# Query norms by transposes instead of matrix products with a column of ones, and small products that are issued at once

## The chip, the core and the metric

The kernel runs on one core of a Trainium2 chip. The metric is the device time of one execution in microseconds (us). Before the change the median of 3 runs is 856.51 us (855.76 to 857.1). The work is split over five engines: TensorE (PE; its weight loads are shown apart as PEld), VectorE (DVE), ScalarE (ACT), GpSimd (POOL) and SyncE (SP, which issues the transfers).

## The reference

One decoder layer: 256 tokens of width 2048, float32, and 256 memory tokens. One input projection gives queries and keys (12 heads of 128 each), values (24 heads of 128), two gate columns per value head, the queries of a cross-attention into the memory tokens, and a SiLU gate of width 4096. The first mixer is a gated DeltaNet; the part that the change touches is its output:

```python
q = jnp.repeat(l2_norm(q), rep, axis=2) * DN_HEAD_DIM ** -0.5
k = jnp.repeat(l2_norm(k), rep, axis=2)
...
o = gated_delta_rule(q, k, v, g, beta)
o = rms_norm(o.astype(p.dtype), out_g)
...
y = jnp.concatenate([mix, xa], axis=-1) * jax.nn.silu(z)
x = x + jnp.einsum("bse,ed->bsd", y, w_out[i])
```

The query enters the delta rule linearly, so its norm can be applied after it: the sum of squares of a query goes into the mean square of the output row by which the output is divided.

## The kernel before, in words

**The stream.** The projections are one long list of weight tiles (`PLAN`): memory values and keys, the gate columns, and then tiles of the kinds x, k, z, v, q and o, 273 in all. Each tile of 512 KB is fetched from memory, rounded by ScalarE to a high part (line 342, `CAST wt<-st`), and VectorE subtracts this from the tile and keeps the rest as a low part (line 346, `wt<-st,wt`). TensorE then multiplies high by high, high by low and low by high (tiles `pa` and `pb` in PSUM; 128x512 or 128x256 products). There are four buffers for prepared tiles (`wt`) and five for raw ones (`st`).

**The small products.** Everything else is a Python generator that runs beside the stream: convolutions, Gram matrices, the inverse of the triangular matrices, the delta rule in six groups of two query heads and four value heads (`delta(g)`), and the transposes of the gated result for the output projection (`split_y`). The builder keeps a clock of its own (`now`) and adds a modelled duration to it for each product (`mm`, `tr`). A generator that wants TensorE next yields `"pe"` with a time, `gather`; it is put on the list `waiting`. After each few products of the stream `step_side` looks at that list: once one entry's time has come, all entries on the list are advanced together. Before, the five requests of a delta group wait up to 0.5 us of the builder's clock for others (`GATHER`), and the transposes of `split_y` up to 4.0 us (`GATHER_Y`). Gram matrices, the cross-attention and the inverse ask with 0.0. Instructions that are issued before 45 us of the builder's clock are pinned to the order of the program; later ones may be moved by the framework's own scheduler, for which the program's order is a rank.

**One delta group.** It takes five rounds on TensorE: (1) keys by keys and queries, `pkq`; (2) the inverse by the first half of the values, `pU`; (3) state products `pU` and the first half's outputs `pO`; (4) the same `pU` and `pO` for the second half; (5) the second half's outputs `pO` and, beside them, the query norms `pqs`. For the norms ScalarE squares the queries of the two heads (`q2`, shown in the trace as `q<-kq`, 128x256 each), and four float32 products with a column of ones sum each over its 128 features: the squared queries are the weights, the column of ones has one column. VectorE reads the four columns from PSUM, adds a small number and scales (`eq`). ScalarE sums the squares of the outputs (`ojunk`), VectorE adds both (`e`), GpSimd raises to the power -1/2, and VectorE scales the outputs and gates them. The PSUM bank of the norms comes from the two banks with the tag `m`.

In the profile every matrix product of the kernel stands under line 86 and nearly every other instruction of the generators under line 103, since helpers issue them. They are told apart by their tiles.

Of the kernel before, what the change touches and what calls it, by code (L numbers as in the profile page):

```python
# [10 lines left out]
AF = mybir.ActivationFunctionType  # L11
ALU = mybir.AluOpType
AX = mybir.AxisListType
# [8 lines left out]
NB = 2  # L22
C = 128
EPS = 1e-6
# [8 lines left out]

LOOK = 2
WARM = 9
GATHER = 0.5
GATHER_Y = 4.0
XPACE = 3.0
HOP = 0.25
PINNED = 45.0  # L40
# [32 lines left out]
def hybrid_kernel(ctx: ExitStack, tc: tile.TileContext, x, xT, memT, W, prm_d, cst_d, out):  # L73
# [32 lines left out]
    def width(ap):  # L106
        n = 1
        for d in ap.shape[1:]:
            n *= d
        return n  # L110
# [14 lines left out]
    ve, se = Engine(nc.vector, ve_cost), Engine(nc.scalar, se_cost)  # L125
# [19 lines left out]
    def S2(name, shape, dt=F32):  # L145
        return s2p.tile([128] + list(shape), dt, name=name, tag="s2")

    def SM(name, shape, bufs=3, dt=F32):
        n = 1
        for d in shape:  # L150
            n *= d
        if n > 128:
            return smp.tile([128] + list(shape), dt, name=name, tag="s1k", bufs=6)
        if n > 16:
            return smp.tile([128] + list(shape), dt, name=name, tag="s512", bufs=3)
        return smp.tile([128] + list(shape), dt, name=name, tag=name, bufs=bufs)
# [7 lines left out]
    def PS(tag, name):  # L164
        idle[tag].remove(min(idle[tag]))
        pt = ps.tile([128, 512], F32, name=name, tag=tag, bufs=PB[tag])
        held[id(pt)] = (tag, pt)
        return pt

    def spare(tag, n=1):  # L170
        return sum(t <= now[0] for t in idle[tag]) >= n

    def give(pt, t):

        idle[held.pop(id(pt))[0]].append(t)

    def bank(tag, name):
        yield from until(lambda: spare(tag))
        return PS(tag, name)

    def banks(name):
        yield from until(lambda: spare("m", 2))
        return [PS("m", name) for _ in range(2)]
# [10 lines left out]
    def mm(o_, lhsT, rhs, start, stop):  # L194
        n = width(rhs)
        if rhs.dtype == F32:
            now[0] += {32: 0.015, 64: 0.038}.get(rhs.shape[0], max(0.19, 4 * n / 2400.0))
        else:
            now[0] += max(0.092, n / 2400.0 + 0.0137) + 0.01 * (n == 256)
        te.matmul(o_, lhsT, rhs, start=start, stop=stop)  # L200

    def tr(o_, i_):
        now[0] += 0.093
        te.transpose(o_, i_, ident)
# [25 lines left out]
    def until(cond):  # L230
        while not cond():
            yield POLL

    def pe_soon(gather=0.0):

        yield max(fin[0] - now[0], 0.0) + SLACK
        yield "pe", gather
# [9 lines left out]
    def calm(queued=CALM):  # L247

        while ve.end > now[0] + queued:
            yield ve.end - now[0] - queued  # L250
# [5 lines left out]
    ones = cst[:, K_ONE : K_ONE + 1]  # L256
# [623 lines left out]
    KQ = [None] * NPAIR  # L880
# [242 lines left out]
    def split_y():  # L1123
        for j0 in (12, 14, 0, 2, 4, 6, 8, 10):
            jj = (j0, j0 + 1)
            yield from until(lambda: all(yf[j] is not None for j in jj))
            yield from calm(0.8)
            yield "pe", GATHER_Y
            pts = yield from banks("pyT")
# [45 lines left out]
    def v_done(g):  # L1175
# [13 lines left out]
        def done(r, pt):  # L1189
            def go():  # L1190
# [41 lines left out]
                if r == 1:  # L1232
                    vss[g] = raw
                    yield from delta(g)
# [8 lines left out]
    def delta(g):  # L1243

        pp = (2 * g, 2 * g + 1)
# [4 lines left out]
        heads = [(w, w // 2, w % 2) for w in range(4)]  # L1250
        yield from pe_soon(GATHER)

# [16 lines left out]
        for i, p in enumerate(pp):  # L1269
            ve.tensor_tensor(out=kcl[:, i], in0=pkv[i][:, 0:4:2, :], in1=kch[:, i], op=ALU.subtract)  # L1270
            give(pks[i], ve.end)
        yield from pe_soon(GATHER)
        A = yield from bank("A", "pU")
# [15 lines left out]
        ve.tensor_tensor(out=ul, in0=u0f, in1=uh, op=ALU.subtract)  # L1289
        yield from pe_soon(GATHER)  # L1290
        yield from until(lambda: spare("A") and spare("B"))
        A, B = PS("A", "pU"), PS("B", "pO")
# [16 lines left out]
        give(B, se.end)  # L1309
        yield from pe_soon(GATHER)  # L1310
        yield from until(lambda: spare("A", 2))
        A, B = PS("A", "pU"), PS("A", "pO")
# [8 lines left out]
        for w in range(4):  # L1321
            se.activation(oq[:, w, :], B[:, w * C : (w + 1) * C], AF.Copy, scale=egc[:, 4 * g + w : 4 * g + w + 1])
        give(B, se.end)
        q2 = S2("q2", [2, 256])
        for i, p in enumerate(pp):
            se.activation(q2[:, i, :], KQ[p][:, 1, :], AF.Square)
        yield from pe_soon(GATHER)
        yield from until(lambda: spare("B") and spare("m"))
        B, pq = PS("B", "pO"), PS("m", "pqs")
        for w, i, h in heads:  # L1330
            mm(B[:, w * C : (w + 1) * C], aT[i][:, 1, h, :], u1[:, w, :], start=True, stop=True)
        for b in range(NB):
            for i in range(2):
                mm(pq[:, 2 * b + i : 2 * b + i + 1], q2[:, i, b * C : (b + 1) * C], ones, start=True, stop=True)
        yield 0.2
        ve.tensor_tensor(out=o[1], in0=B.rearrange("c (h e) -> c h e", h=4), in1=oq, op=ALU.add)
        give(B, ve.end)

        eq, e4 = SM("eq", [4], 2), SM("e4", [3, NB, 4], 2)
        ve.tensor_scalar(out=eq, in0=pq[:, 0:4], scalar1=EPS, scalar2=EPS * 128, op0=ALU.add, op1=ALU.mult)  # L1340
        give(pq, ve.end)
        ready.add(f"d{g}")
        yield
        for b in range(NB):
            for w in range(4):
                junk = SM("ojunk", [C])
                se.activation(junk, o[b][:, w, :], AF.Square, accum_out=e4[:, 0, b, w : w + 1])
        yield
        yield from until(lambda: {f"z{g}0", f"z{g}1"} <= ready)
        ev = [e4[:, a].rearrange("c b (i h) -> c (b i) h", h=2) for a in range(2)]  # L1350
        ve.scalar_tensor_tensor(out=ev[1], in0=ev[0], scalar=1.0 / 128,
# [156 lines left out]
```

## Time and profile before

| | before |
|---|---|
| median of 3 runs | 856.51 us (855.76 to 857.1) |
| the profiled execution, its own time | 857.04 us |
| its span, first to last instruction | 855.3 us |
| PE busy | 848.0 us, 99% |
| PE weight loads busy | 709.7 us, 83% |
| DVE busy | 618.1 us, 72% |
| ACT busy | 538.1 us, 63% |
| POOL busy | 46.5 us, 5% |
| instructions | 13175, of them 4790 matrix products |

Busy time is the union of the intervals in which an engine has an instruction under way. Products on TensorE overlap, so one shown with 390 ns can be followed by the next after 230 ns: what a product costs is read from the starts of two neighbours, not from its duration. A float32 product (two passes) stands in the trace as two records with a weight load each, a transpose as one record.

### The profile page before, as it was taken

The numbers are of one execution on the slowest core, as the hardware profiler recorded it, in microseconds if no ns is written. First come the engines' busy times: TensorE is split into PE (matmuls) and PEld (weight loads), VectorE is DVE, ScalarE is ACT, GpSimd is POOL, SyncE is SP. The second block draws the span as 40 slices with busy tenths as digits, with TensorE's granted clock in tenths as the row PEclk, the third lists the DMA queues.
The fourth block names the chain that finished last, engine by engine and source line by source line (L and its number), as shares of the span: only waits on it lengthen the run. The fifth ranks groups of instructions, "written<-read, shape, count | busy, mean of one in ns | idle before, by whom it ended". The sixth has DMA issues, their size and how long they took to land.

```text
span 855.3 us, 13175 instructions
## 1 busy us (share of the span) xinstructions
PE 848.0 (99%) x4790; PEld 709.7 (83%) x4790; DVE 618.1 (72%) x1080; ACT 538.1 (63%) x929; POOL 46.5 (5%) x45
## 2 busy tenths in 40 slices
PE   9999999999999999999999999999999999999998
PEld 6888888888888888888888888788888888888886
DVE  6878886657779974788889989568886655454442
ACT  7656665798644765995966676679775654333331
POOL 1000000000000000001100202000010000000000
PEclk9999999999999999999999999999999999999999
DMA  9965566448677886869877769686755547666650
GB/s 344 335 218 177 171 189 165 146 147 263 197 208 241 263 243 180 261 210 266 226 243 218 227 214 279 198 242 222 227 158 169 186 142 265 214 210 205 199 197 25
DMA packets 145433, 181.59 MB, mean 212 GB/s; under 512 B 24824, under 2 KB 115824, under 8 KB 145368
## 3 DMA queue, kind: packets, MB, share of 16 engines
q1 hardware_dynamic: 145080, 180.47, 67.0%
q8 instruction: 37, 0.61, 0.3%
q10 hardware_dynamic: 288, 0.28, 0.1%
q14 instruction: 28, 0.23, 0.1%
HBM read 167.58 MB, written 6.89 MB: 204 GB/s over the span
## 4 chain that ended last, share of the span: by engine, by line
PE 95%; ACT 2%; DMA 1%; DVE 1%; issue 1%; SPq 0%; DVEq 0%
PE pb L86 72%; PE pa L86 13%; PE pO L86 2%; PE pU L86 2%; PE pm L86 1%; PE pkq L86 1%; PE pyT L86 1%; ACT dec L103 1%; DVE wt L346 1%; PE pqs L86 1%; PE pkk L86 1%; DMA erow<-dgc 0%; DMA st<-W_d 0%; ACT L103 0%; PE pab L86 0%
## 5 line engine op out<-in xcount | busy, mean ns | idle before, releaser
L346 DVE TENSOR_TENSOR wt<-st,wt 128x1024 fp32r<-128x1024 f32 (+1 forms) x275 | 331.9, 1212 | 164.9 <-ACT wt L342 161.2
L342 ACT CAST wt<-st 128x1024 fp32r<-128x1024 f32 (+1 forms) x275 | 286.3, 1045 | 224.3 <-PE pb L86 180.6
L86 PE MATMUL pb<-wt,hkt 128*128 128x512 f32 x1536 | 361.8, 392 | 0.0
L86 PEld LDWEIGHTS pb<-wt,hkt 128*128 128x128 f32 x1536 | 284.7, 188 | 58.7 <-DVE wt L346 0.4
L86 PE MATMUL pb<-wt,yhi 128*128 128x512 f32 x512 | 158.0, 390 | 0.0
L86 PE MATMUL pa<-hkt,wt 128*128 128x512 f32 (+1 forms) x768 | 142.8, 342 | 0.4 <-DVE wt L346 0.3
L86 PEld LDWEIGHTS pa<-hkt,wt 128*128 128x128 f32 x768 | 117.9, 188 | 18.3 <-DVE wt L346 1.0
L86 PEld LDWEIGHTS pb<-wt,yhi 128*128 128x128 f32 x512 | 95.7, 188 | 19.6
L86 PE MATMUL pb<-wt,ylo 128*128 128x512 f32 x256 | 99.7, 389 | 0.0
L86 PE MATMUL pb<-wt,mkt 128*128 128x512 f32 x384 | 88.6, 391 | 0.9 <-ACT wt L342 0.9
L86 PEld LDWEIGHTS pb<-wt,mkt 128*128 128x128 f32 x384 | 71.6, 188 | 16.8 <-ACT wt L342 1.8
L86 PEld LDWEIGHTS pb<-wt,ylo 128*128 128x128 f32 x256 | 48.1, 188 | 10.1
L103 ACT ACT_TABLE_LOAD x31 | 39.8, 1283 | 1.4 <-DVE acc L103 1.0
L103 DVE SCALAR_TENSOR_TENSOR acc<-raw,prm,acc 128x255 f32<-128x255 f32 (+2 forms) x72 | 34.2, 476 | 3.6 <-ACT acc L103 3.2
L103 DVE TENSOR_TENSOR inT<-inXT,inN 96x1 f32<-96x1 f32 (+22 forms) x92 | 29.1, 342 | 3.2 <-DMA inN<-dN 2.4
L103 DVE TENSOR_REDUCE inXT<-inT 96x1 f32<-96x1 f32 (+22 forms) x92 | 28.6, 337 | 0.7
L103 POOL TENSOR_TENSOR e<-e,mhalf 128x8 f32<-128x8 f32 x6 | 20.8, 3472 | 120.5 <-DVE e L103 120.5
L103 DVE TENSOR_TENSOR vc<-vc 128x512 f32<-128x512 f32 x36 | 24.5, 682 | 0.1
L103 POOL TENSOR_TENSOR srk<-skt,mhalf 128x4 f32<-128x4 f32 x6 | 7.0, 1175 | 224.6 <-DVE skt L103 145.6
L103 DVE SCALAR_TENSOR_TENSOR o<-o,e,zs 128x128 f32<-128x128 f32 x48 | 14.0, 345 | 7.0 <-POOL e L103 7.0
L103 ACT ACTIVATE ojunk<-o 128x128 f32<-128x128 f32 x48 | 14.4, 301 | 7.0 <-DVE o L103 4.9
L103 DVE TENSOR_TENSOR vc<-vc,vw 128x512 f32<-128x512 f32 x24 | 16.4, 683 | 2.8 <-DMA vc<-vs 2.8
(202 smaller groups left out, 693.9 us busy)
## 6 DMA issues: line engine op xcount, KB each, us to landing
st<-W_d SPq DMA_DIRECT2D x271, 512.0 KB
erow<-dgc SPq DMA_DIRECT2D x24, 256.0 KB
vw<-dtap SPq DMA_DIRECT2D x24, 256.0 KB
dN<-dec SPq DMA_DIRECT2D x12, 256.0 KB
n<-dN SPq DMA_DIRECT2D x12, 256.0 KB
vc<-vs SPq DMA_DIRECT2D x12, 224.0 KB
vc<-vc SPq DMA_DIRECT2D x12, 224.0 KB
xraw<-xT_d SPq DMA_DIRECT2D x8, 256.0 KB
```

The source lines that it names most:

```text
L86: return lambda *a, **k: pin(getattr(self.eng, op)(*a, **k))
L103: return pin(getattr(self.eng, op)(*a, **k))
L342: pin(se.eng.copy(hi[:, w] if parts > 1 else hi, st[:, w] if parts > 1 else src))
L346: pin(ve.eng.tensor_tensor(out=lo[:, w] if parts > 1 else lo, in0=st[:, w] if parts > 1 else src, in1=hi[:, w] if parts > 1 else hi, op=AL ...
```

## The change

The query norms of a delta group are made another way. The queries themselves are transposed (four transposes of 128x128 into one bank of PSUM, `pqT`), ScalarE squares the whole bank in one instruction of 512 columns, and VectorE sums each run of 128 columns in one reduction. The two squares ahead of round 5 are gone, and so are the four float32 products with the column of ones. The addition and the scaling of `eq` come after the sums of the outputs' squares now, and read SBUF, not PSUM. The PSUM bank is released by ScalarE and no longer by VectorE. `GATHER` goes from 0.5 to 0.0 and `GATHER_Y` from 4.0 to 0.5.

```diff
-GATHER = 0.5
-GATHER_Y = 4.0
+GATHER = 0.0
+GATHER_Y = 0.5
...
-        q2 = S2("q2", [2, 256])
-        for i, p in enumerate(pp):
-            se.activation(q2[:, i, :], KQ[p][:, 1, :], AF.Square)
         yield from pe_soon(GATHER)
         yield from until(lambda: spare("B") and spare("m"))
-        B, pq = PS("B", "pO"), PS("m", "pqs")
+        B, pq = PS("B", "pO"), PS("m", "pqT")
         for w, i, h in heads:
             mm(B[:, w * C : (w + 1) * C], aT[i][:, 1, h, :], u1[:, w, :], start=True, stop=True)
-        for b in range(NB):
-            for i in range(2):
-                mm(pq[:, 2 * b + i : 2 * b + i + 1], q2[:, i, b * C : (b + 1) * C], ones, start=True, stop=True)
+        for w in range(4):
+
+            tr(pq[:, w * C : (w + 1) * C], KQ[pp[w % 2]][:, 1, w // 2 * C : (w // 2 + 1) * C])
         yield 0.2
         ve.tensor_tensor(out=o[1], in0=B.rearrange("c (h e) -> c h e", h=4), in1=oq, op=ALU.add)
         give(B, ve.end)
 
         eq, e4 = SM("eq", [4], 2), SM("e4", [3, NB, 4], 2)
-        ve.tensor_scalar(out=eq, in0=pq[:, 0:4], scalar1=EPS, scalar2=EPS * 128, op0=ALU.add, op1=ALU.mult)
-        give(pq, ve.end)
+        q2 = S2("q2", [4, C])
+        se.activation(q2.rearrange("c w e -> c (w e)"), pq, AF.Square)
+        give(pq, se.end)
         ready.add(f"d{g}")
         yield
...
         yield
+        ve.tensor_reduce(out=eq, in_=q2, axis=AX.X, op=ALU.add)
+        ve.tensor_scalar(out=eq, in0=eq, scalar1=EPS, scalar2=EPS * 128, op0=ALU.add, op1=ALU.mult)
         yield from until(lambda: {f"z{g}0", f"z{g}1"} <= ready)
```

## Rows read from the trace of the kernel before

**Rows 1.** The page's busy times by engine, and the TensorE clock granted in 40 slices of the span, in tenths of full speed.

```profile
PE 848.0 (99%) x4790; PEld 709.7 (83%) x4790; DVE 618.1 (72%) x1080; ACT 538.1 (63%) x929; POOL 46.5 (5%) x45
...
PEclk9999999999999999999999999999999999999999
```

**Rows 2.** The chain of work that ended last: the page's shares by engine, and from its pieces (start us, us, what) those of the end, from 690 us on.

```profile
PE 95%; ACT 2%; DMA 1%; DVE 1%; issue 1%; SPq 0%; DVEq 0%
...
712.81 138.75 PE pb L86 x612
```

**Rows 3.** All waits of PE (engine, line, what it waited for: us in total, times, longest us), over the whole span.

```profile
PE warm L86 <- DVE warm L103: 1.2, 1, 1.2
PE pm L86 <- issue: 1.0, 2, 0.8
PE pb L86 <- ACT wt L342: 0.9, 1, 0.9
PE pa L86 <- DVE wt L346: 0.3, 1, 0.3
```

**Rows 4.** The timeline of PE from 691 us on (start us, us, engine, line, operation, tiles and shapes, count): the fifth round of the last delta group, and a pair of the transposes of `split_y`, both between products of the output projection.

```profile
691.13 0.39 PE L86 MATMUL pb<-wt,ylo 128*128 128x512 f32 x1
691.36 1.05 PE L86 MATMUL pO<-u,aT 128*128 128x128 f32 x8
692.24 0.95 PE L86 MATMUL pqs<-cst,q 128*128 128x1 f32 x8
693.06 0.72 PE L86 MATMUL pb<-wt,yhi 128*128 128x512 f32 x2
693.62 0.40 PE L86 MATMUL pb<-wt,ylo 128*128 128x512 f32 x1
...
697.05 0.39 PE L86 MATMUL pb<-wt,ylo 128*128 128x512 f32 x1
697.29 1.03 PE L86 MATMUL pyT<-cst,o 128*128 128x128 f32 x8
698.08 0.71 PE L86 MATMUL pb<-wt,yhi 128*128 128x512 f32 x2
698.62 0.39 PE L86 MATMUL pb<-wt,ylo 128*128 128x512 f32 x1
```

**Rows 5.** The timeline of the weight loads in the same stretch: the eight loads of the norms and the two of the stream behind them.

```profile
692.13 0.97 PEld L86 LDWEIGHTS pqs<-cst,q 128*128 128x128 f32 x8
693.03 0.30 PEld L86 LDWEIGHTS pb<-wt,yhi 128*128 128x128 f32 x2
```

**Rows 6.** Groups of PE's instructions by tiles and shape (count | busy us, mean ns of one | idle before): the norms and the transposes of the outputs, over the whole span.

```profile
L86 PE MATMUL pyT<-cst,o 128*128 128x128 f32 x48 | 6.2, 272 | 0.0
L86 PE MATMUL pqs<-cst,q 128*128 128x1 f32 x48 | 5.9, 238 | 0.0
```

**Rows 7.** Groups of VectorE: the reduction that the Gram matrices make, 512 columns into 4; and from the instructions on the tile `eq` the step that reads the norms (count: duration ns min/median/max, first and last start us).

```profile
L103 DVE TENSOR_REDUCE skt<-dg 128x4 f32<-128x512 f32 x6 | 4.1, 684 | 0.2
...
L103 DVE TENSOR_SCALAR eq<-pqs x6: 143/152/163, 408.4 to 693.2; 128x4 f32<-128x4 f32 x6
```

**Rows 8.** Groups of ScalarE: the squares of the queries, a square of 512 columns in another part of the kernel (from SBUF), and SiLU of 512 columns read from PSUM.

```profile
L103 ACT ACTIVATE zs<-pb 128x512 f32<-128x512 f32 x16 | 9.3, 593 | 1.9 <-PE pb L86 1.8
...
L103 ACT ACTIVATE msq<-mst 128x512 f32<-128x512 f32 x8 | 4.8, 618 | 0.0
...
L103 ACT ACTIVATE q<-kq 128x256 f32<-128x256 f32 x12 | 4.5, 440 | 0.0
```

**Rows 9.** Busy us (and instructions) of each engine in the stretches in which the six groups end, granted clock, share of the DMA engines, GB/s.

```profile
400.00:425.00 25.00, 25.00 (x120) 20.63 (x119) 21.58 (x41) 23.96 (x58) 3.80 (x5) 1.00 0.89 252
455.00:470.00 15.00, 15.00 (x92) 13.26 (x91) 14.96 (x32) 9.61 (x23) 0.52 (x1) 1.00 0.62 196
515.00:530.00 15.00, 15.00 (x94) 13.18 (x93) 15.00 (x29) 8.40 (x21) 0.52 (x1) 1.00 0.95 299
610.00:630.00 20.00, 20.00 (x108) 17.15 (x107) 19.96 (x33) 13.05 (x25) 0.00 (x0) 1.00 0.46 141
640.00:655.00 15.00, 15.00 (x85) 12.78 (x84) 8.34 (x13) 10.01 (x26) 1.64 (x1) 1.00 0.57 175
685.00:700.00 15.00, 15.00 (x80) 12.73 (x79) 8.30 (x16) 8.40 (x18) 1.64 (x1) 1.00 0.34 109
```

**Rows 10.** Waits of ScalarE's rounding of weight tiles for TensorE (to give a buffer back), from 455 to 530 us.

```profile
ACT wt L342 <- PE pa L86: 9.6, 5, 3.5
ACT wt L342 <- PE pb L86: 8.0, 8, 2.5
```

**Rows 11.** Waits of the weight loads over the whole span, those for tiles of the stream and of the delta groups.

```profile
PEld pa L86 <- DVE wt L346: 1.0, 2, 0.6
...
PEld pb L86 <- DVE wt L346: 0.7, 3, 0.3
...
PEld pO L86 <- ACT u L103: 0.5, 2, 0.3
...
PEld pqs L86 <- ACT q L103: 0.2, 1, 0.2
```

**Rows 12.** The timeline of PE from 404 us on: the fifth round of the first delta group.

```profile
404.87 1.16 PE L86 MATMUL pO<-u,aT 128*128 128x128 f32 x8
405.78 0.71 PE L86 MATMUL pb<-wt,hkt 128*128 128x512 f32 x2
406.34 0.28 PE L86 MATMUL pqs<-cst,q 128*128 128x1 f32 x2
406.48 0.71 PE L86 MATMUL pb<-wt,hkt 128*128 128x512 f32 x2
407.02 0.72 PE L86 MATMUL pqs<-cst,q 128*128 128x1 f32 x6
```

**Rows 13.** The timeline of all engines from 446 us on, the second delta group: the copy that fills `u`, and the products of round 5 that read it.

```profile
456.80 0.59 ACT L103 COPY u<-pU 128x512 f32<-128x512 f32 x1 [2.14 <-DVE inXT L103]
...
461.34 1.05 PE L86 MATMUL pO<-u,aT 128*128 128x128 f32 x8
```

## The prediction

> **What bounds the kernel now.** I began with the page's busy times and the granted clock. PE is busy for 848.0 us of a span of 855.3 us, and the clock is at its upper level, 2.4 GHz, in all 40 slices [rows 1]. Busy time of a pipelined engine can hide idle array time, so I went on to the chain that ended last: 95% of it is PE, and its last piece is 612 products of the output projection in 138.75 us, one every 0.2267 us [rows 2]. Then to PE's waits, which come to 3.4 us in all, 1.2 of them for the warm-up tile at the very start [rows 3]. The reader is to see in these three views that TensorE works nearly without a hole. So the time is the sum of what TensorE is given to do, and two questions are left: how much TensorE time the change takes out, and whether the reordered rest opens holes.
>
> **The change part by part.** *The four products with the column of ones go.* They stand as 8 records in each of six groups, 48 in all [rows 6]. Their 238 ns each are no price, since records overlap. The price comes from the starts of the stream's products around a burst. From the `ylo` product at 691.13 to the next at 693.62 us are 2.49 us [rows 4]. In these lie three products of the stream (that one and two `yhi`), 3 x 0.2267 = 0.68 us, and 16 small records, which therefore cost 1.81 us, 0.113 us each. The eight norms alone: their first weight load starts at 692.13 and the stream's next at 693.03 us, so 0.90 us [rows 5]. Six groups: 5.4 us. That a record of one column costs as much as one of 128 says that the weight load, 128 columns in both, is what is paid for.
>
> *Four transposes come.* A burst of eight such transposes lies between the `ylo` products at 697.05 and 698.62 us: 1.57 us, less 0.68 us for three products of the stream, is 0.89 us or 0.111 us each [rows 4]. Four cost 0.445 us, six groups 2.67 us. Each group thus gives back 0.90 - 0.445 = 0.455 us, all six **2.7 us**. As to the bounds: the nearest other price for a transpose is that of the float32 records, 0.113 us, which makes 2.71 us for the 24 and a gain of 2.7 us again; a start that isn't overlapped could add at most the 0.272 us which one transpose lasts [rows 6], in each group, 1.6 us, leaving a gain of 1.1 us. I take 2.7, since in every burst read the neighbours overlap.
>
> The Trainium skill, in "TensorE: Matmul & The Clock Gate", section "Back-to-back issue gap", has a table that sets the pace by columns: about 60 cycles for 1 to 64 columns and 134 for 128, at the upper clock. An estimate from that page is 8 x 60 / 2.4 = 0.20 us for the norms and 4 x 134 / 2.4 = 0.22 us for the transposes, so that nothing would be gained and 0.1 us lost over six groups. The trace disagrees for passes that each load weights: eight of them took 0.90 us [rows 5].
>
> *ScalarE.* Two squares of 256 columns at 440 ns go, one of 512 comes, read from PSUM. The nearest rows are 618 ns (a square from SBUF) and 593 ns (from PSUM) [rows 8]. By busy time 4.5 us go and 6 x 0.6 = 3.6 us come. The squares stood ahead of the norms on TensorE, where they caused a wait of 0.2 us [rows 11]; the transposes need only the queries, which are there long before. ScalarE is nearly full in one of the six stretches, 23.96 of 25 us [rows 9], so the 0.15 us a group helps there if anything.
>
> *VectorE.* Per group one reduction of 512 columns into 4 comes, 684 ns like that of the Gram matrices; the step on `eq` stays, 152 ns, and reads another memory [rows 7]. That is 6 x 0.68 = 4.1 us more. It is hidden if the prepared weight tiles stay ahead of TensorE. In three of the six stretches VectorE has no time left (14.96 of 15, 15.00 of 15, 19.96 of 20 us) [rows 9]. But from 455 to 530 us, which holds two of them, ScalarE waited 17.6 us of 75 for TensorE to give a buffer back [rows 10]: preparation runs ahead there and is throttled by the buffers. I take nothing as its cost; without cover it is 3 x 0.68 = 2.1 us. The chain of the group behind it (`e`, the power, the gating) gets 0.7 us longer, and nobody waits: the stream goes on.
>
> *The PSUM bank of the norms* comes free after a square on ScalarE rather than a 152 ns step on VectorE. Both queue behind similar work; a later `m` bank delays small products only. Nothing, with a bound of one square, 0.6 us, in each of six groups to the bad, and as much to the good, if VectorE's queue was the longer one.
>
> *The two gather times.* Waiting for company would pay if entering and leaving the stream cost something. From the same rows: 16 records in one burst cost 0.113 us each, the eight transposes alone 0.111 us. So an extra entry costs no more than a few hundredths of a microsecond. A group asks five times, 30 in all; 30 more entries at 0.02 us would be 0.6 us. Products that are asked for 0.5 us sooner may also reach TensorE before their inputs, which is the rival below. Mostly there is room: in the second group `u` was copied by 457.39 us and is read at 461.34 [rows 13]. Besides, the order isn't the builder's alone: four norms that the program issues in a row stand in the trace as two records, two products of the stream, and six more [rows 12]. I take nothing for the gather times, between -1.5 us (waits in the groups that happen to go) and +0.6 us. The moved `eq` steps pass no transfers; no DMA is added or moved.
>
> **The sum.** 857.04 us (the profiled execution, 1.7 us of it outside the span) - 5.4 + 2.7 = 854.3 us. The median of the runs is 0.53 us below that execution, so for a median 856.51 - 2.7 = **853.8 us**, 0.3% less.
>
> **The rivals.** *More goes than the products* (chance 0.13). The weight loads' waits for the stream's tiles from VectorE, for `u` and for the squares come to 1.0 + 0.7 + 0.5 + 0.2 = 2.4 us [rows 11]. If a calmer ScalarE and another order take 1.5 us of these away, the time is 852.3. Against it: none of the causes but the 0.2 us is removed on purpose.
>
> *VectorE takes it back* (0.17). In the three full stretches [rows 9] the reduction pushes each subtraction behind it by 0.68 us, and TensorE meets late tiles: 2.1 us, so 856.51 - 2.7 + 2.1 = 855.9 us. For it: 1.7 us of waits for such tiles exist now [rows 11]. Against it: the buffers' waits [rows 10].
>
> *Slower: small products stand at the head of TensorE's queue before their inputs* (0.12). TensorE takes its instructions in order, so a product that comes 0.5 us sooner and finds its input unfinished holds the whole stream. The place is the 30 requests of the delta groups. If each waits half of the 0.5 us, they lose 7.5 us: 856.51 - 2.7 + 7.5 = 861.3 us. It eats up the gain from 2.7 / 30 = 0.09 us a request on. For it: twice a round's product already waited for `u`, 0.5 us together [rows 11]. Against it: the 4 us of room in [rows 13], and that the scheduler put products of the stream between where it thought an input late [rows 12].
>
> *The pace follows the columns* (0.03). The stream's pace is 0.2267 us for 512 columns; were columns all that counts, a transpose of 128 would cost 0.057 us and a product of one column next to nothing, so 24 transposes add 1.36 us and the 48 records give back 0.02: 857.8 us. This is what the table cited above amounts to in this kernel. Against it stands the 0.90 us for eight one-column passes [rows 5].
>
> *The gather times change nothing in the real order*, since the scheduler reorders anyway [rows 12]: then that half of the change doesn't do what it says, and the time is that of the forecast, because I put it at nothing. It has no chance of its own.
>
> **How the numbers follow.** The forecast has 0.55, the others 0.13, 0.17, 0.12 and 0.03. What a measurement of this kernel can tell from no change is about 0.2%, 1.7 us, so "faster" is below 854.8. It holds 0.53 of the forecast's 0.55 (its own spread is about 852.9 to 854.9), the 0.13, and 0.04 of the VectorE case, where one full stretch of three would pay: 0.70. "Same" holds 0.02 of the forecast, 0.13 of the VectorE case, 0.03 of the early products (under 0.15 us each) and 0.02 of the last: 0.20. "Slower" gets 0.09 + 0.01 = 0.10. The range for 8 in 10 reaches from 851.8 (all 2.4 us of waits gone would be 851.4) to 856.8 (the VectorE case with the uncertain 0.6 us for entries and a little more), and leaves out most of the early products and the last case.
>
> **What would show each step.** Right: no `pqs` records, 24 records `pqT<-` whose neighbours start 0.11 us apart, 4766 products in all; PE's busy time down by nearly 3 us; from the start of the last transposes to the end the same 138.75 us for 612 products; PE's waits still some 3 us. The reduction at 0.68 us, six times, and ScalarE's waits for TensorE's buffers still there. Wrong: waits of `pO`, `pU` or `pkq` for `u`, `uh`, `vc` or `kq` that sum to microseconds (early products), more waits of PE or its weight loads for VectorE's `wt` between 400 and 630 us (VectorE), or bursts of `pqT` that take over 0.6 us for four (the price of a transpose). A time under 851 us would mean that the gather times had a price I didn't see.

## The result and the profile after

The changed kernel takes 860.49 us in the median of 8 runs (858.75 to 861.85), the kernel before 857.16 us in 8 runs on the same chip (855.76 to 857.61). The ratio is 1.0036, with a 95% interval of 1.0025 to 1.0047: slower by some 3.1 us, where 2.7 us less were forecast. The time lies outside the range, on the other side.

The profiled execution of the changed kernel took 861.61 us (before: 857.04), its span is 859.8 us (855.3). First the page: the busy times (before in [rows 1]) and the shares of the chain that ended last (before in [rows 2]).

```profile
PE 848.7 (99%) x4766; PEld 709.5 (83%) x4766; DVE 621.9 (72%) x1086; ACT 537.2 (62%) x923; POOL 45.1 (5%) x45
...
PE 81%; DVE 5%; issue 4%; DMA 4%; ACT 3%; POOL 1%; SPq 0%; DVEq 0%; POOLq 0%; ACTq 0%
```

Two things are to be seen. PE has the 4766 products that were announced, 24 fewer. But its idle time (span less busy time) is 859.8 - 848.7 = 11.1 us, where it was 855.3 - 848.0 = 7.3 us, and the chain runs over other engines in a fifth of the span, not in a twentieth.

What was taken out of TensorE did go. The same piece of the timeline of PE as in [rows 4], in the changed kernel (start us, us, engine, line, operation, tiles and shapes, count):

```profile
692.78 0.39 PE L86 MATMUL pb<-wt,ylo 128*128 128x512 f32 x1
693.00 1.05 PE L86 MATMUL pO<-u,aT 128*128 128x128 f32 x8
693.89 0.60 PE L86 MATMUL pqT<-cst,kq 128*128 128x128 f32 x4
694.25 0.71 PE L86 MATMUL pb<-wt,yhi 128*128 128x512 f32 x2
694.80 0.40 PE L86 MATMUL pb<-wt,ylo 128*128 128x512 f32 x1
```

From one `ylo` product to the next are 694.80 - 692.78 = 2.02 us; before they were 2.49 us with the same three products of the stream. The group gives back 0.47 us; 0.455 were forecast. The other five groups look the same: from the first of the four transposes to the next product's start are 0.35 to 0.36 us in all six, where the eight norm records took 0.81 us before in the four groups that have them in a row, so some 2.7 us went in all. Behind the last delta group nothing changed either: the last piece of the chain is 636 products in 144.19 us, 0.2267 us each, as in [rows 2].

The new steps, in the groups by shape (count | busy us, mean ns of one | idle before):

```profile
L86 PE MATMUL pqT<-cst,kq 128*128 128x128 f32 x24 | 3.6, 273 | 0.0
L103 DVE TENSOR_REDUCE eq<-q 128x4 f32<-128x512 f32 x6 | 4.1, 677 | 0.4 <-ACT q L103 0.4
L103 ACT ACTIVATE q<-pqT 128x512 f32<-128x512 f32 x6 | 3.6, 593 | 3.4 <-PE pqT L86 3.3
```

Reduction and square cost what was forecast (0.68 and 0.6 us). So the loss is in what stood under "nothing". The waits of PE (before in [rows 3]; engine, line, what it waited for: us in total, times, longest us):

```profile
PE pb L86 <- DVE wt L346: 1.7, 2, 1.4
PE pm L86 <- ACT Y L103: 1.7, 1, 1.7
PE pb L86 <- ACT wt L342: 1.4, 2, 0.8
PE warm L86 <- DVE warm L103: 1.2, 1, 1.2
PE pU L86 <- DVE ul L103: 0.6, 1, 0.6
PE pa L86 <- DVE wt L346: 0.3, 1, 0.3
PE pm L86 <- ACT Am L103: 0.2, 1, 0.2
```

Seven groups where four stood before, 7.1 us for 3.4. They are not spread over the kernel. Three of the following stretches hold nearly all of the difference in idle time: windows of the changed kernel, and then the same of the kernel before (from:to us, length, then busy us and count of PE, PEld, DVE, ACT, POOL, the granted clock, DMA share, GB/s).

```profile
0.00:20.00 20.00, 18.01 (x63) 12.67 (x64) 13.26 (x23) 15.72 (x26) 4.20 (x7) 1.00 0.91 343
400.00:440.00 40.00, 38.26 (x180) 31.09 (x179) 36.01 (x75) 34.44 (x73) 5.28 (x5) 1.00 0.83 250
500.00:520.00 20.00, 19.30 (x99) 15.91 (x98) 16.78 (x32) 14.26 (x24) 0.00 (x0) 1.00 0.64 199
540.00:580.00 40.00, 37.46 (x480) 30.90 (x481) 23.80 (x40) 28.57 (x54) 5.29 (x3) 0.96 0.71 223
```

```profile
0.00:20.00 20.00, 17.90 (x70) 12.44 (x71) 12.84 (x23) 15.45 (x25) 4.20 (x7) 1.00 0.91 340
400.00:440.00 40.00, 40.00 (x191) 32.91 (x190) 34.46 (x71) 36.72 (x80) 3.80 (x5) 1.00 0.81 244
500.00:520.00 20.00, 20.00 (x110) 17.27 (x109) 19.69 (x37) 12.19 (x25) 0.52 (x1) 1.00 0.72 224
540.00:580.00 40.00, 38.95 (x492) 31.74 (x492) 23.17 (x32) 29.41 (x54) 1.03 (x2) 1.00 0.72 230
```

PE stands idle 1.74 us from 400 to 440 us where it was never idle, 0.70 us from 500 to 520 where it was never idle, and 2.54 instead of 1.05 us from 540 to 580: 3.9 us more, which is the page's whole difference in idle time (3.8). In the last stretch the granted clock is lower too. And in the first 20 us PE does 63 products instead of 70 in the same busy time; that is 7 x 0.2267 = 1.6 us, and more on it stands in the last section.

**From 540 to 580 us** lies the merge of the second half of the inverse: short products (`pm`) in four rounds, and between the rounds ScalarE copies their results from PSUM (`Am`, `XN`, `Y`, `A`). The timeline of PE in the changed kernel, after the second round:

```profile
552.93 2.33 PE L86 MATMUL pb<-wt,hkt 128*128 128x512 f32 x9
556.99 0.33 PE L86 MATMUL pm<-Y,n 64*64 64x64 f32 x2 [1.73 <-ACT Y L103]
...
559.54 2.83 PE L86 MATMUL pm<-A,XN 64*64 64x64 f32 x48
562.30 0.91 PE L86 MATMUL pb<-wt,hkt 128*128 128x512 f32 x2
```

Nine products of the stream cover the copies, and then the third round waits 1.73 us for `Y`. The timelines of ScalarE say why, the changed kernel first, then the kernel before at the same place:

```profile
553.09 1.28 ACT L103 ACT_TABLE_LOAD   x1
554.38 0.63 ACT L103 ACTIVATE dec<-dec 128x512 f32<-128x512 f32 x1
555.02 0.95 ACT L103 COPY XN<-pm 32x384 f32<-32x384 f32 x2
555.99 1.93 ACT L103 COPY Y<-pm 32x384 f32<-32x384 f32 x4
```

```profile
548.45 1.28 ACT L103 ACT_TABLE_LOAD   x1
549.74 0.63 ACT L103 ACTIVATE dec<-dec 128x512 f32<-128x512 f32 x1
551.53 0.95 ACT L103 COPY XN<-pm 32x384 f32<-32x384 f32 x2 [1.16 <-PE pm L86]
552.50 1.94 ACT L103 COPY Y<-pm 32x384 f32<-32x384 f32 x4
```

The same four steps, in another place: before, the table load and the `dec` step were done while the second round still ran, and ScalarE stood waiting for its end (1.16 us); after, they stand between the round and its copies. Neither belongs to the norms. Their cost is the same and their place is not.

Behind this wait the clock falls. A window of the changed kernel around the last 48 short products (columns as above):

```profile
559.30:562.60 3.30, 3.30 (x57) 3.18 (x54) 0.94 (x1) 2.87 (x9) 0.38 (x1) 0.50 0.25 72
```

In these 3.30 us the granted clock is 0.50, the lower level of 1.2 GHz, and PE counts as busy in all of them, so no wait shows what it costs. The 48 products `pm<-A,XN` last 2.83 us here; in `after_v6_second`, a run further down whose granted clock is 1.00 at this place, the same 48 last 1.61 us:

```profile
557.11 1.61 PE L86 MATMUL pm<-A,XN 64*64 64x64 f32 x48
```

That is 1.2 us measured. If all that ran in the 3.30 us was slowed to half, 1.65 us are lost; this estimate is used below.

**From 400 to 440 us** the 1.41 us of the longest wait lie before 424.19 us, for a tile that VectorE prepares. Its timeline in the changed kernel:

```profile
418.81 1.14 DVE L103 SCALAR_TENSOR_TENSOR o<-o,e,zs 128x128 f32<-128x128 f32 x4 [1.54 <-POOL e L103]
...
422.91 2.36 DVE L346 TENSOR_TENSOR wt<-st,wt 128x1024 fp32r<-128x1024 f32 x2
```

The gating `o` of a finished group was at the head of VectorE's queue before GpSimd had the power `e`; VectorE stood 1.54 us, then did a row of short steps, and only at 422.91 us the next tile. **From 500 to 520 us** the rival of the early products shows itself in one place: PE has `pU` at the head of its queue and waits 0.63 us for `ul`, which VectorE only then subtracts.

```profile
515.20 0.39 PE L86 MATMUL pU<-ul,kch 128*128 128x256 f32 x1 [0.63 <-DVE ul L103]
```

The sum: -2.7 (products) + 3.8 (idle time) + 1.65 (clock, the estimate) + 1.6 (start) = +4.35 us, of 4.5 us by which the spans differ.

### The profile page after: what moved, and what is told of

Read it like the earlier page. It is cut to its first block, busy times and chain, and to the rows that moved or that the text cites. A ratio compares the mean times of both kernels' runs of the same rounds, so it can differ in the third digit from the quotient of the medians.

```text
span 859.8 us, 13127 instructions
## 1 busy us (share of the span) xinstructions
PE 848.7 (99%) x4766; PEld 709.5 (83%) x4766; DVE 621.9 (72%) x1086; ACT 537.2 (62%) x923; POOL 45.1 (5%) x45
## 4 chain that ended last, share of the span: by engine, by line
PE 81%; DVE 5%; issue 4%; DMA 4%; ACT 3%; POOL 1%; SPq 0%; DVEq 0%; POOLq 0%; ACTq 0%
PE pb L86 62%; PE pa L86 11%; DVE wt L346 2%; PE pO L86 1%; PE pU L86 1%; DMA st<-W_d 1%; DMA erow<-dgc 1%; POOL e L103 1%; PE pm L86 1%; ACT dec L103 1%; PE pkq L86 1%; PE pyT L86 1%; DMA vc<-vs 1%; DVE acc L103 1%; DVE vc L103 1%
## 5 line engine op out<-in xcount | busy, mean ns | idle before, releaser
L103 ACT ACTIVATE dec<-erow,gcc 128x128 f32<-128x128 f32 x48 | 16.5, 396 | 5.6 <-DMA erow<-dgc 5.5
L103 ACT COPY raw<-pa 128x512 f32<-128x512 f32 x24 | 13.9, 583 | 6.5 <-PE pa L86 6.1
```

The lines of the kernel that those rows point to most:

```text
L103: return pin(getattr(self.eng, op)(*a, **k))
```

## The experiments

Three causes were to be told apart. *The gather times* put small products at the head of TensorE's queue before their inputs. *The norms* cost VectorE or ScalarE more than they give TensorE. *The order*: the framework's scheduler lays out all the engines' work behind 45 us, and any difference in the program's order or in an instruction makes it lay out what follows differently, so that the loss belongs to none of the parts by its own work. Each ratio is to the kernel before, measured beside it on the same chip, with its 95% interval; us are ratio less 1, times the 857 to 858 us of before.

**The two halves alone.** `norms_only` has the diff of the norms and the old gather times. The other three have the old norms:

```text
 g0_only:  GATHER = 0.0, GATHER_Y = 4.0
 gy_only:  GATHER = 0.5, GATHER_Y = 0.5
 g0_gy:    GATHER = 0.0, GATHER_Y = 0.5
```

> The new norms with the two gather times as before (0.5 and 4.0). Gather theory (the losses come from products that are issued at once): TensorE's work falls by 2.7 us and nothing new stalls, 854.4 us against 857.2. VectorE theory (the reduction, 0.68 us a group, makes weight tiles late): the losses near 400 to 424 and 500 to 520 us stay, about 3.5 us, and the time is 857 to 858. Order theory (any edit makes the scheduler's order another one, and each order has stalls of its own): between 854 and 860, with stalls in other places than in the changed kernel.

> The kernel before with the delta groups' gather time 0.0, the norms and the transposes' 4.0 as before. Gather theory: the stalls of the changed kernel near 409 to 424, 514 and 549 to 562 us come with it, 5 to 6 us, so 862 to 863 us. VectorE theory: no change, 857. Order theory: 855 to 862, stalls at new places.

> The kernel before with the gather time of the output's transposes 0.5, all else as before. Every theory: the first of these transposes come at 592 us, after the stalls, so no change, 857 us, and the order before 580 us is that of before.

> The kernel before with both gather times of the change and the norms as before. Gather theory: as the one with 0.0 alone, 862 to 863 us, that is the changed kernel plus its 2.7 us. VectorE theory: 857. Order theory: not the sum of the parts.

| | median us | ratio | us |
|---|---|---|---|
| norms_only | 865.54 | 1.0084 (1.007 to 1.0097) | +7.2 |
| g0_only | 861.84 | 1.0041 (1.0025 to 1.0058) | +3.5 |
| gy_only | 857.25 | 0.9997 (0.9985 to 1.0008) | -0.3 |
| g0_gy | 862.21 | 1.0044 (1.0032 to 1.0056) | +3.8 |

The parts don't add: 7.2 + 3.8 is 11 us, and the whole change costs 3.1. The norms, which take 2.7 us of work away, are alone the dearest. And the causes change with the kernel. Some waits of PE in `g0_only`:

```profile
PE pb L86 <- DVE wt L346: 1.4, 2, 0.9
PE pO L86 <- ACT u L103: 1.3, 1, 1.3
...
PE pqs L86 <- ACT q L103: 1.2, 1, 1.2
```

and in `norms_only`:

```profile
PE pb L86 <- issue: 3.1, 1, 3.1
PE pyT L86 <- DVE o L103: 1.8, 1, 1.8
```

In `g0_only` early products are real: `pO` waits for `u`, and the norms `pqs` for ScalarE's squares `q`, 1.2 to 1.3 us, once each, and 2 us behind the second the granted clock falls to 0.50. With the transposes the second of these can't occur; by the ratios the whole change is 0.7 us faster than `g0_gy`, but the two intervals overlap. `g0_only` also has 1.4 us of waits for late weight tiles, before 409 and 418 us, in the stretch where the changed kernel has its 1.41 us, and it has no reduction. In `norms_only` the merge is hit again, at another time, with a hole of 3.1 us for which the profile has no releaser; its cause stays open. And the transposes of the outputs, `pyT`, wait 1.8 us for the gated output `o`, the end of the chain in which the reduction now stands. The same wait is in `after_v12` and `norms_v12` further down, which have the new norms too, and in no other run. How much of it the reduction makes, and how much the order, was not tried.

**The order alone.** Two other pairs of gather times, with the old norms and with the new ones: a quarter and 2.0 between the two tried, and 1.0, twice the old `GATHER`.

```text
 old_q, new_q:  GATHER = 0.25, GATHER_Y = 2.0
 old_1, new_1:  GATHER = 1.0,  GATHER_Y = 4.0
```

> Old norms, gather times 0.25 and 2.0: the same instructions as before in another order. Order theory (each order that the scheduler deals has stalls of its own, and the one before has few): slower than before by stalls alone, 858 to 863 us, with TensorE's own work at the 837.3 us of before. VectorE theory (the reduction is what hurts): 857.

> New norms, gather times 0.25 and 2.0. Order theory: work 834.5 us, stalls unrelated to those of the partner with the old norms, between 854 and 866 us. VectorE theory: slower than the partner with the old norms, by stalls for weight tiles behind the reduction.

> Old norms, gather times 1.0 and 4.0. Order theory: as for 0.25, 858 to 863 us. VectorE theory: 857. A theory in which waiting for company pays in itself: no slower than before.

> New norms, gather times 1.0 and 4.0. Order theory: between 854 and 866 us; over the four pairs with equal gather times the mean of new less old is near the 2.8 us of saved work, with a scatter of several us. VectorE theory: slower than its partner.

| | median us | ratio | us |
|---|---|---|---|
| old_q | 864.8 | 1.0088 (1.0058 to 1.0118) | +7.5 |
| new_q | 865.16 | 1.0086 (1.0063 to 1.011) | +7.4 |
| old_1 | 865.66 | 1.0089 (1.0063 to 1.0115) | +7.6 |
| new_1 | 868.09 | 1.012 (1.0086 to 1.0154) | +10.3 |

`old_q` lies between two gather times that cost nothing and 3.5 us, and costs 7.5 itself. `old_1` lets products wait longer, so that fewer are early, and costs as much. No price of a request and none of an early product explains both. What is left, with the same products in both, is the order. The difference of the new norms to the old at equal gather times, by the ratios, is +7.2 us (0.5 and 4.0), -0.7 (0.0 and 0.5), -0.2 and +2.7, where the work alone would give -2.7 each time. Their mean is +2.2 us and not near -2.7; with so wide a scatter four pairs can't tell whether the norms cost something of their own besides the order. The places, by `old_q`'s waits of PE, are known: `Y` in the merge as in the changed kernel, and the squares as in `g0_only`.

```profile
PE pm L86 <- ACT Y L103: 3.2, 2, 2.5
PE pqs L86 <- ACT q L103: 2.4, 1, 2.4
```

**The merge's copies on VectorE.** If the wait for `Y` and the clock behind it are some 3 us of the loss, moving the copies away from ScalarE should win them. `after_v6` is the changed kernel with the six copies of the second round (`XN` and `Y`) on VectorE in both merges; `after_v12`, `before_v12` and `norms_v12` move all thirteen, in the changed kernel, the kernel before and `norms_only`; `after_v6_second` moves the six in the second merge alone.

```diff
-            se.copy(xall[64 * e + 32 : 64 * e + 64, e, :, 0:32], x21[at(e, 0)])
-        give(pms[1], se.end)
+            ve.tensor_copy(xall[64 * e + 32 : 64 * e + 64, e, :, 0:32], x21[at(e, 0)])
+        give(pms[1], ve.end)
...
```

> The changed kernel, with six of ScalarE's copies between the rounds of the inverse's merge (XN and the first four of Y, 0.47 us each, 2.85 us per merge) made by VectorE. ScalarE theory (near 550 us ScalarE is full, its copies and weight roundings come late, TensorE stands idle and its clock halves): TensorE's wait for Y goes, the clock stays up, and 3 to 4 us come back: 856 to 857.5 us. Order theory (every edit deals another order, and its stalls fall anywhere): 855 to 866 us, with the wait for Y perhaps gone and others in its place.

> The changed kernel with all copies of the merge on VectorE (5.7 us per merge from ScalarE). ScalarE theory: the loss between 540 and 580 us, 5.3 us in the changed kernel, falls below that of before (3.1), so 855 to 857 us. Order theory: 855 to 866 us.

> The kernel before with all copies of the merge on VectorE. ScalarE theory: its loss of 3.1 us between 540 and 580 us halves, 855.5 to 857 us. Order theory: slower than before like every other order of the old norms with a changed gather time of the delta groups, 860 to 866 us.

> The new norms with the gather times of before and all copies of the merge on VectorE. ScalarE theory: the stall of 6.4 us near 584 us goes, the waits after 700 us stay (4 us): 857 to 860 us. Order theory: 855 to 866 us.

> The changed kernel with six copies of the second merge alone made by VectorE; its order is that of the changed kernel up to about 550 us. If the loss near 550 us is ScalarE's late copies and the halved clock behind them: the wait for Y goes, the clock stays up, and 3 us come back less what the order behind it brings, 857 to 858.5 us. If not: 860.5 us.

| | median us | ratio | us |
|---|---|---|---|
| after_v6 | 861.17 | 1.004 (1.0025 to 1.0056) | +3.4 |
| after_v12 | 866.53 | 1.0095 (1.0071 to 1.0119) | +8.1 |
| before_v12 | 867.24 | 1.0105 (1.0081 to 1.0129) | +9.0 |
| norms_v12 | 866.93 | 1.0095 (1.0065 to 1.0124) | +8.1 |
| after_v6_second | 857.46 | 0.9998 (0.9985 to 1.0011) | -0.2 |

An edit at both merges is again an edit of the order from the first merge on: `after_v6` loses nothing in the second merge in its profiled execution (the fastest of ten, 858.51 us), but 3.0 us before 356.88 us, where `pkq` waits for `kq`, and moving all thirteen costs 8 to 9 us whatever the norms are.

```profile
PE pkq L86 <- ACT kq L103: 3.0, 1, 3.0
```

The last one changes the order only from about 550 us on, and that is the test. Its windows (columns as above):

```profile
400.00:440.00 40.00, 38.19 (x176) 30.97 (x175) 35.38 (x74) 33.78 (x71) 5.28 (x5) 1.00 0.80 247
...
540.00:580.00 40.00, 39.24 (x499) 32.12 (x498) 29.85 (x51) 27.87 (x50) 3.75 (x3) 1.00 0.83 257
```

From 400 to 440 us the loss is as in the changed kernel, from 540 to 580 us PE is idle for 0.76 instead of 2.54 us and the clock stays up, and the kernel is 3.3 us faster by the two ratios. That is the idle time and the clock, 1.78 + 1.65 = 3.4 us; from the intervals the 3.3 us are known to about 1.5 us. This part of the cause is shown. The rest adds up too: less work, 2.7 us, against idle time that is 1.8 us more than before from 400 to 440 us, 0.45 us more from 500 to 520 and 0.3 us less in the merge leaves some -0.7 us, and -0.2 (-1.3 to +0.9) was measured.

**How early the order changes.** The new norms in some groups only, the others as before; gather times as before.

```diff
+        new = g == 0
+        if not new:
...
```

This is `norms_g0`, the first group alone; `norms_g2`, `norms_g3` and `norms_g4` have `g >= 2`, `g >= 3` and `g >= 4` in its place.

> The new norms in the first of the six delta groups alone, gather times as before: one reduction and one square more than before, 0.45 us less work for TensorE, and the order of the instructions on TensorE differs from 400 us on. Order theory: 859 to 866 us, as with the new norms in all groups. VectorE theory (each reduction costs): about a sixth of what all six cost, 857 to 858.5 us.

> The new norms in groups 2 to 5: 1.8 us less work, order of before up to about 520 us, so the merge near 550 us comes in a new order. Order theory: the merge decides, 854.5 us where it stays as before, 858 to 862 where TensorE waits there over a microsecond and the clock halves. VectorE theory: fallen with the first group alone.

> The new norms in groups 3 to 5 alone: three reductions, 1.4 us less work, and the order of before up to about 615 us, so through the merge near 550 us. Order theory: no new stalls up to 615 us and then whatever the new order brings, 855.5 to 860 us. VectorE theory: half of what all six cost, 860 to 861 us.

> The new norms in groups 4 and 5 alone: 0.9 us less work, the order of before up to about 648 us. Order theory: 856 to 860 us. VectorE theory: 859 to 860 us. If neither costs anything: 856.3 us.

The second column says from where on the products of the stream and the small ones come in another sequence than before (worked out from the order of PE's records in the two traces), the third what the work alone gives.

| | order differs from | work alone, us | median us | ratio | us |
|---|---|---|---|---|---|
| norms_g0 | 400 us | -0.45 | 861.78 | 1.0037 (1.0025 to 1.0049) | +3.2 |
| norms_g2 | 520 us | -1.8 | 857.58 | 0.9999 (0.9988 to 1.001) | -0.1 |
| norms_g3 | 615 us | -1.35 | 856.48 | 0.9981 (0.9967 to 0.9994) | -1.6 |
| norms_g4 | 648 us | -0.9 | 857.8 | 0.9989 (0.9979 to 1.0) | -0.9 |

One group, with one reduction more on VectorE, loses 3.2 us; three and two late groups, with three and two reductions, give what their work says. `norms_g2` lies between, 1.7 us above its work; in its window from 540 to 580 us PE is idle for 2.13 us, twice as long as before. That late groups cost nothing doesn't speak for the order alone, since VectorE is half idle where the last two groups end [rows 9]. What decides is where `norms_g0` loses. The windows of `norms_g3` first, in which the order is still that of before:

```profile
400.00:440.00 40.00, 40.00 (x190) 32.95 (x189) 34.48 (x71) 36.69 (x80) 3.76 (x5) 1.00 0.83 245
...
540.00:580.00 40.00, 39.72 (x497) 32.45 (x497) 23.10 (x33) 29.39 (x55) 1.03 (x2) 1.00 0.71 225
```

and then that of `norms_g0`, which has the kernel before's norms in all groups but the first:

```profile
540.00:580.00 40.00, 36.44 (x475) 29.21 (x474) 21.64 (x32) 28.00 (x53) 1.03 (x2) 0.96 0.73 229
```

PE is idle for 3.56 us around the merge, more than 100 us behind the one changed group, where no norm of any kind is changed, and the clock falls again. The merge is a place that the old order happens to pass well. One caution on single profiles: with the order still that of before, `norms_g3` has 0.28 us of idle time from 540 to 580 us where before had 1.05, and a wait of 1.07 us for a weight tile before 589.71 us where before had none. So a stall of about 1 us can come and go from one execution to the next.

**Both that helped together.** `g3_v6_second` is `norms_g3` with the six copies of the second merge on VectorE.

> The new norms in groups 3 to 5 and six copies of the second merge made by VectorE; order of before up to about 550 us. If ScalarE's late copies are what costs there: 1 us less than with the norms alone, 855 to 856 us. Order theory: 855 to 860 us, by what the order behind 550 us brings.

It takes 863.74 us, ratio 1.0071 (1.0055 to 1.0088): +6.1 us. By its waits of PE the loss lies elsewhere once more: 1.8 us for `q` before 614 us, and 2.1 us for `ylo` and 1.7 us for `yhi` in the output projection, which comes too early for them.

What helps one order does not help another. `norms_g3` stays the fastest, and the only one whose interval lies wholly under 1. Of the expectations by the order theory, eight came out too low (`norms_only`, `old_q`, `old_1`, `new_1`, the three with thirteen copies moved, and `g3_v6_second`): it says that a new order has stalls, but not how many.

## Why the prediction was wrong

- *The work of TensorE.* Right: 0.47 us in the group shown where 0.455 was forecast, 2.7 us in all, and the two late partial versions agree with it (1.6 us, 0.5 to 2.8, for three groups; 0.9 us, 0.0 to 1.8, for two).
- *ScalarE, VectorE, the bank of the norms.* Sizes right (593, 677 ns). That VectorE's work is hidden is borne out in the late groups: `norms_g3` has three of the six reductions, one of them in a stretch in which VectorE was full, and no loss. The rival that VectorE takes it back, as forecast in the three full stretches, doesn't fit `norms_g0`: its one reduction lies in none of them, and it loses 3.2 us, mostly at the merge. For the second and third group, both in full stretches, the rival isn't excluded (`norms_g2`). Its sign, more waits for VectorE's `wt`, did come, 1.7 us in the changed kernel, but `g0_only` has 1.4 us of them at the same place without a reduction. The 1.41 us wait before 424 us hangs on the chain `eq`, `e`, power, gating, in which the reduction makes `e` later; how much of the wait is that, against the place of `o` in VectorE's queue, wasn't tried. "Nobody waits" for that chain was in any case wrong: VectorE stood 7.0 us for the power even before the change (8.2 us after, the page's group of `o`), and in `norms_only` TensorE itself waits 1.8 us for the chain's end.
- *The gather times.* This is the step that failed first: "I take nothing for the gather times, between -1.5 us (waits in the groups that happen to go) and +0.6 us". `g0_only` measured +3.5 us (2.1 to 5.0) for `GATHER`; `GATHER_Y` alone is nothing (-1.3 to +0.7). The price isn't that of 30 entries to the stream, which the bound was made from. In `g0_only` it is a wait of 1.3 us, one of 1.2 us with the lower clock behind it, and 1.4 us for late tiles, each at a place where the new order puts a step behind others on its engine or a product ahead of its input. In the changed kernel what stood at nothing came to 3.8 us of idle time and, by the estimate, 1.65 us at the lower clock; 3.3 us of that are the merge's, by `after_v6_second`.
- *The same failure in the norms.* The sum took the order of all the rest as given. I wrote that "the order isn't the builder's alone" and drew from it only that the edit might do little. The other reading is the right one: the scheduler lays out everything behind the edit anew. `norms_only` was to give -2.7 us by my sum and gave +7.2.
- *The rivals.* "Early products" had the right sign and size of time (861.3 us against 860.49), but by luck: not 30 requests at 0.25 us, but one of 0.63 us in the changed kernel, where most of the loss is late tiles, the merge and the clock. Its mechanism is at work in `g0_only`, twice. The transposes take one kind of early product away. "The pace follows the columns" is refuted by the 0.47 us. "The gather times change nothing in the real order" is refuted by `g0_only`, whose order differs from before's from 366 us on.
- *The chances.* 0.10 for slower came from asking what each part costs. That other orders of the same work cost 0.4 to 0.9% (`g0_only`, `g0_gy`, `old_q`, `old_1`; `before_v12`, with thirteen copies a merge on another engine, 1%) couldn't be read from one trace, but the page's 99% busy could have told which way a disturbance goes: with 3.4 us of waits in all there is little to gain from another order and much to lose.

Open: why the hole of 3.1 us in `norms_only` (3.9 us in `norms_v12`) follows a run of the merge's short products with no releaser in the profile; why the order of before is so much better than nearly all the others; whether the new norms cost something of their own in the early groups; and what the norms would give with the order held to that of before in all six groups, which wasn't tried.

## What to carry to other kernels

Where a scheduler orders the work and the busiest engine has no hole, price an edit as its own work plus a new order of all that follows it, and find the spread of the second by edits that change no work (here +3.5 to +7.6 us from 366 or 388 us on, more than the edit's 2.7, and -0.3 us for `gy_only`, which changes the order from 636 us on). Put such an edit as late in the program as it still pays, or hold the order ahead of the tight places fixed (which was not tried): the same norms gained 1.6 us in the last three groups and lost 7.2 in all six. Late is no guarantee: `g3_v6_second` changes the order from about 554 us on and loses 6.1 us. Look for the tight places first: here a chain that goes from short products through ScalarE copies and back, with an engine's unrelated long steps free to slip in between.

## What the hardware showed unexpectedly

**Behind a stall of 1.7 us amid short products the clock fell.** In the changed kernel the granted clock is 0.50 in the 3.30 us from 559.30 us on, 2.3 us behind the end of the merge's wait. In `g0_gy` PE waited 1.5 us for `q`, and just behind it the window shows the same, with products of the stream only (columns as above):

```profile
529.80:533.10 3.30, 3.30 (x13) 2.81 (x12) 3.30 (x6) 0.21 (x2) 0.00 (x0) 0.50 0.63 215
```

Products of 512 columns start 0.42 us apart in it, where 0.227 us is the pace elsewhere, so the 1.5 us of waiting were followed by a loss of about as much again, and a stall was not over when its releaser came. Not each stall does this, and its length alone doesn't decide: behind the 1.41 us before 424 us of the changed kernel the clock stayed up, as the window from 400 to 440 us shows, and so it did behind the 3.0 us for `kq` in `after_v6` (granted clock 1.000 over the whole span). The Trainium skill, "TensorE: Matmul & The Clock Gate", section "A second HAM failure mode: psum-queue depth-cycling", tells of a kernel in which frequent small idle spells between groups of products made the clock swing between its two levels. The trace agrees in that the clock fell behind idle spells of 1.5 and 1.73 us, but here a single spell came before each fall. By `after_v6_second`, which has neither that wait nor the fall, the pair cost 3.3 us here.

**The start differs from one execution to the next.** From the first weight tile on PE does 14 products in the changed kernel's profiled execution in the time in which it did 21 before (timelines of PE, after and then before):

```profile
6.02 5.17 PE L86 MATMUL pb<-wt,mkt 128*128 128x512 f32 x14 [0.78 <-ACT wt L342]
```

```profile
6.12 5.17 PE L86 MATMUL pb<-wt,mkt 128*128 128x512 f32 x21 [0.89 <-ACT wt L342]
```

At 5.17 / 14 = 0.37 us a product it ran for a good part at the lower clock. The trace's record of the granted clock begins at the full level, at 9.73 us in this execution and at 5.24 us in that of before (the windows' 1.00 ahead of that is no record); from 6.02 us up to there the products start every 0.427 us, and then every 0.227 us. The change touches nothing there: `norms_only`, with the same instructions up to that point, has 10 products in the window from 8 to 10 us where the changed kernel has 7 and before 11. So 1.6 us of the 4.5 us between the two profiled spans belong to these executions, and what is left, 2.9 us, fits the 3.1 us of the medians. The Trainium skill says the same of the number of products at the lower clock at a kernel's start, on the same page, section "Part 1: The HAM clock gate": it differs from run to run.
